# Conditioning slices of a two-layer hybrid backbone: where their bias is loaded and where the odd layer sums them

## The chip, the cores and the metric

The kernel runs on one core of a Trainium2 chip. The number is the device time of one execution in microseconds (us), and the time before is the median of three executions. A core has five engines with a queue of instructions each: TensorE (PE, with its weight loads PEld), VectorE (DVE), ScalarE (ACT), GpSimd (POOL) and SyncE (SP). An engine works through its queue in order. Transfers run on 16 DMA engines; in this kernel SP issues the large loads and POOL the small ones, those that spread a row over partitions, and the indirect ones.

## The reference, cut to what matters

```
for l in range(2):
    sh1, sc1, g1, sh2, sc2, g2 = split(silu(c) @ ada_w[l] + ada_b[l], 6)
    u = rmsnorm(x, norm1_g[l]) * (1 + sc1) + sh1
    y = even_mixer(u, u_ctx, ...) if l == 0 else odd_mixer(u, ...)
    x = x + g1 * (y @ w_out[l])
    x = x + g2 * hier_moe(rmsnorm(x, norm2_g[l]) * (1 + sc2) + sh2, ...)
```

512 tokens of width 1024, in fp32. The even mixer is neighbourhood attention beside a short gated convolution; the odd mixer is Hyena (two long convolutions, each with a gate) beside a Conformer convolution with a layer norm. The MoE picks one of four groups and two of its four experts. `ada_w[l]` is 1024 x 6144: the six conditioning slices of a layer cost 24 MB of weights for one vector c (the context's vector goes through layer 0 beside it), and of them the gate g1 and the three of the MoE are wanted only when the mixer's out-projection ends.

## The kernel before, in words

The program is written for a framework that orders each engine's instructions itself, by a timeline that it estimates, with the order of the program text as priority. So an instruction can move in its engine's queue when others around it do.

**Projections.** A weight chunk of 128 x 1024 is loaded (`raw`), split into a high part by a cast on ACT (`whi`, line 141) and the rest by a subtraction on DVE (`wlo`, line 142), and every product is three matmuls (`mm3`, lines 155 to 157). `proj_ch` makes 128 channels for all 512 tokens, 24 matmuls. The parts lie in a pool `wp` of four slots each.

**Conditioning.** The slices are made in pairs j = 0, 1, 2 of 2048 columns. `ada` does a pair with matmuls. `ada_sums` does it without PE: for each half h of the columns, eight loads of 512 KB are multiplied by a column of silu(c) and added up on DVE into `adaacc` (lines 245 and 247), and two matmuls with a column of ones per half then sum the partitions into a PSUM tile `ps` (line 253). After the second half `ada_done` adds the bias (line 266, tile `adar`), multiplies in a norm's gain (line 311), and stores four rows to DRAM (`adad`, line 271). For layer 0 pairs 1 and 2 go this way, between the attention's query projections; for layer 1 pairs 1 and 2, as a generator `fill` of 20 steps (ten a pair: two loads and their additions are a step, the products end a step, the last step is the bias and the store). In layer 1 the loads (`adaw`) take `whi` and `wlo` slots of `wp`.

**The bias tile.** After the last product the bias is loaded by POOL into a tile `adab` of tag `t2` (lines 256 to 258; 128 x 512, each of four rows spread over 32 partitions). Tag `t2` has four buffers, which the norm's `y` tiles and others use too.

**The odd layer's order.** `ORDER` (line 63) is a list of steps: `p`, `v`, `x` are Hyena projections with a short convolution, `c` a Conformer block (two projections, the gate `sg`, a shifted copy `wide` by 16 transfers at line 815, 31 matmuls at line 819), `A` and `B` long convolutions (transforms at lines 629 and 800), `L` the layer norm; `t` followed by a number takes that many steps of `fill`. In the list before, 18 of the 20 steps come ahead of `B0` and the last two after `B1`.

**What waits for the last pair.** `mid` (line 938) loads the stored rows again, spread over the partitions, by POOL (`bcast`, line 317): g1b and b2b for the residual, a2b and g2b from pair 2, and `ab` (line 973) for the router. `evac` (lines 1018 and 1019) adds g1 times the out-projection to the residual `xr`; line 997 scales it by a2b for the MoE (`hm`); `wa` (line 981) is the router's weight scaled by pair 2, which the logits (line 1037) need; line 1026 transposes `xr` for them.

Of the kernel before, what the change touches and what calls it, by code (L numbers as in the profile page):

```python
# [8 lines left out]
F32 = mybir.dt.float32  # L9
# [37 lines left out]
FW = [0.5, 0]  # L47
GD = 0
DE = [[], []]
BK = 0  # L50
PB = (4, 2, 2)
SX = 1
FB = 4
# [6 lines left out]
PM = 1  # L60
PU = [[], []]
FIRST = (640, 128)
ORDER = 'p1 t1 v1 t1 v0 t1 p0 t1 c0 t2 A0 v3 t1 v2 t1 p2 t1 c2 t2 p3 t1 c1 t2 A1 x0 t1 c3 t2 x1 t1 B0 x2 L0 x3 B1 t9'
TWO_PI = (6.28125, 0.0019350051879882812, float(2.0 * math.pi - 6.28125 - 0.0019350051879882812))
P_, Q_ = (0, 1, 2, 3), (4, 5, 6, 7)
NP1, NP2, NQ2, NQ3 = 8, 9, 10, 11
# [2 lines left out]
class Build:  # L69
# [83 lines left out]
    def mm3(self, ps, lh, ll, rh, rl, first, last):  # L153
        nc = self.nc
        nc.tensor.matmul(ps, lh, rh, start=first, stop=False)  # L155
        nc.tensor.matmul(ps, lh, rl, start=False, stop=False)  # L156
        nc.tensor.matmul(ps, ll, rh, start=False, stop=last)  # L157

    def proj_tok(self, uh, ul, W, t, ks=range(8), at=8, mid=None):

# [10 lines left out]
    def proj_ch(self, uh, ul, w, c0, lo_engine=None):  # L171

        v3 = lambda r: r.rearrange("p (k c) -> p k c", k=8)
        raw = self.raw_load(w[c0 // 128])
        wh, wl = self.split(v3(raw), lo_engine)
        ps = self.mmt()
        for k in range(8):
            self.mm3(ps, wh[:, k, :], wl[:, k, :], uh[k], ul[k], k == 0, k == 7)
        return ps

    def rstd(self, ss, n, eps, name):
# [25 lines left out]
    def ada(self, l, j):  # L207

        nc, A = self.nc, self.A
        b = A["ada_b"]  # L210
        ps = self.mmt()
        for k in range(8):
            if k == BK:
                bias = self.wk.tile([128, 512], F32, tag="t2", name="adab")
                nc.gpsimd.dma_start(bias, bass.AP(tensor=b.tensor, offset=b.offset + l * 6144 + j * 2048,
                                                  ap=[[512, 4], [0, 32], [1, 512]]))
            raws = []
            for h in range(2):
                raws.append(self.spare.pop(0) if self.spare else self.rawp.tile([128, 1024], F32, tag="raw", name="raw"))
                if self.spare:  # L220
                    self.spare.append(raws[-1])
                c0 = j * 2048 + h * 1024
                nc.sync.dma_start(raws[-1], A["ada_w"][l, k * 128:k * 128 + 128, c0:c0 + 1024])
            for g in range(4):
                nc.tensor.matmul(ps[32 * g:32 * g + 32, :], self.cT[:, k, :],
                                 raws[g // 2][:, (g % 2) * 512:(g % 2) * 512 + 512], start=(k == 0), stop=(k == 7))
            yield
        self.ada_done(l, j, ps, bias)

    def ada_sums(self, l, j):  # L230

        nc, A = self.nc, self.A
        b = A["ada_b"]
        for h in range(2):
            acc = self.ep2.tile([128, 1024], F32, tag="adaacc", name="adaacc", bufs=1)
            c0 = j * 2048 + h * 1024
            for k in range(8):
                if l and j:
                    raw = self.wp.tile([128, 1024], F32, tag=("whi", "wlo")[k % 2], name="adaw")
                else:  # L240
                    raw = self.spare.pop(0)
                    self.spare.append(raw)
                nc.sync.dma_start(raw, A["ada_w"][l, k * 128:k * 128 + 128, c0:c0 + 1024])
                if k == 0:
                    nc.vector.tensor_scalar(acc, raw, self.cT[:, k, 0:1], None, op0=ALU.mult)
                else:
                    nc.vector.scalar_tensor_tensor(acc, raw, self.cT[:, k, 0:1], acc, op0=ALU.mult, op1=ALU.add)
                if k % 2:
                    yield
            if not h:  # L250
                ps = self.mmt()
            for g in (2 * h, 2 * h + 1):
                nc.tensor.matmul(ps[32 * g:32 * g + 32, :], self.onec.to_broadcast([128, 32]), acc[:, (g % 2) * 512:(g % 2) * 512 + 512],
                                 start=True, stop=True)
            if not h:
                yield
        bias = self.wk.tile([128, 512], F32, tag="t2", name="adab")
        nc.gpsimd.dma_start(bias, bass.AP(tensor=b.tensor, offset=b.offset + l * 6144 + j * 2048,
                                          ap=[[512, 4], [0, 32], [1, 512]]))
        self.ada_done(l, j, ps, bias)  # L260
        yield

    def ada_done(self, l, j, ps, bias):
        nc, A = self.nc, self.A
        rows = self.ep2.tile([128, 512], F32, tag="adar", name="adar", bufs=1)
        nc.vector.tensor_tensor(rows, ps, bias, op=ALU.add)
        if j == 0:
            self.gain_rows(A["norm1_g"], l, 64, rows)
        elif j == 2:
            self.gain_rows(A["norm2_g"], l, 0, rows)  # L270
        nc.sync.dma_start(self.adad[l][j], rows[0:128:32, :])
        if j == 0:
            self.cols[l] = self.cp.tile([128, 16, 1], F32, name=f"adac{l}")
            nc.sync.dma_start(self.cols[l].rearrange("p a o -> p (a o)"),
                              self.adad[l][j].rearrange("a (q p) -> p (a q)", p=128))
# [549 lines left out]
    def odd(self, st):  # L825
# [82 lines left out]
        fill = self.ada1  # L908
        for w in ORDER.split():
            if w[0] == "t":  # L910
# [669 lines left out]
```

## Time and profile before

| | us |
|---|---|
| median of three executions (lowest, highest) | 1089.05 (1087.94, 1095.08) |
| the profiled execution's own time | 1094.75 |
| its span in the trace | 1092.9 |
| PE busy | 994.9 |
| DVE busy | 799.6 |
| ACT busy | 500.0 |
| POOL busy | 237.4 |

The span leaves 1.85 us of the profiled execution's time outside. Times in the trace count from the start of the span. The mean granted clock of TensorE is 0.947 of full speed: the clock falls to half in stretches, mostly behind a wait of PE. The odd layer runs up to about 840 us and the second MoE from there on.

### The profile page before, as it was taken

The page shows a single profiled execution, that of the slowest core. Times are in us where ns is not written, and L with a number is a line of the kernel's source. Part 1 is how long each engine was busy: PE and PEld are TensorE (multiplying, and loading weights), DVE is VectorE, ACT ScalarE, POOL GpSimd, SP SyncE. Part 2 cuts the span into 40 slices and gives each one's busy share as a digit, 9 for nine tenths or more (in the row PEclk, how much of TensorE's full clock was granted, in tenths as well). Part 3 has the DMA queues.
Part 4 walks back from the last instruction along what each step waited for, and adds up shares of the span by engine and source line. Part 5 has one row for each costly group of instructions (what it writes and reads, how often), then busy time and mean ns, then how long its engine had stood idle before and what let it go on. Part 6 is the DMA issues. An engine that isn't in the chain of part 4 may idle for free.

```text
span 1092.9 us, 14537 instructions
## 1 busy us (share of the span) xinstructions
PE 994.9 (91%) x5070; PEld 747.1 (68%) x5070; DVE 799.6 (73%) x1215; ACT 500.0 (46%) x786; POOL 237.4 (22%) x245
## 2 busy tenths in 40 slices
PE   6999999989995899999977999998998949999995
PEld 4787777667884677777755757566576837777663
DVE  3584588487368798898958787867755368988894
ACT  4342313477244576568624413212153137676562
POOL 2030313011343232353320000000011131333221
PEclk8999989989998899999988999998989779999998
DMA  9965783752624779999645755636227685799885
GB/s 350 345 215 161 245 277 116 267 182 95 214 93 175 260 244 340 309 313 299 195 148 195 256 153 175 201 79 211 77 100 241 241 289 194 242 293 323 306 256 139
DMA packets 77989, 240.78 MB, mean 220 GB/s; under 512 B 17987, under 2 KB 19806, under 8 KB 77912
## 3 DMA queue, kind: packets, MB, share of 16 engines
q1 hardware_dynamic: 62488, 209.83, 55.6%
q0 software_dynamic: 15424, 29.98, 11.1%
q8 instruction: 41, 0.67, 0.3%
q14 instruction: 36, 0.29, 0.1%
HBM read 227.40 MB, written 25.73 MB: 232 GB/s over the span
## 4 chain that ended last, share of the span: by engine, by line
PE 69%; DMA 11%; DVE 10%; issue 5%; ACT 2%; SPq 1%; POOL 1%; POOLq 0%; DVEq 0%; ACTq 0%
PE mm L155 15%; PE mm L156 15%; PE mm L157 14%; PE mm L1420 4%; PE mm L819 4%; DVE wlo L142 3%; DMA adab<-in_ada_b 2%; PE tr L1372 2%; DMA adaw<-in_ada_w 2%; PE mm L629 2%; PE mm L575 1%; DMA raw<-in_moe 1%; DMA xe<-hd,gi 1%; PE sc L545 1%; PE sc L629 1%
## 5 line engine op out<-in xcount | busy, mean ns | idle before, releaser
L141 ACT CAST whi<-raw 128x1024 fp32r<-128x1024 f32 x199 | 206.3, 1051 | 146.4 <-PE mm L156 46.0
L142 DVE TENSOR_TENSOR wlo<-raw,whi 128x1024 fp32r<-128x1024 f32 x199 | 242.4, 1229 | 35.0 <-ACT whi L141 34.3
L155 PE MATMUL mm<-whi,xt 128*128 128x512 f32 x208 | 85.7, 412 | 0.5 <-ACT xt L1375 0.5
L156 PE MATMUL mm<-wlo,xt 128*128 128x512 f32 x208 | 84.1, 404 | 1.8 <-DVE wlo L142 1.5
L157 PE MATMUL mm<-whi,xt 128*128 128x512 f32 x208 | 82.8, 398 | 0.0
L1361 POOL DMA_INDIRECT xe<-hd,gi x34 | 44.0, 1293 | 115.8 <-PE tr L1372 101.5
L156 PE MATMUL mm<-u,whi 128*128 128x512 f32 x160 | 64.1, 401 | 2.0 <-DVE u L349 2.0
L155 PE MATMUL mm<-u,whi 128*128 128x512 f32 x160 | 63.9, 408 | 1.1 <-ACT u L345 0.7
L157 PE MATMUL mm<-u,wlo 128*128 128x512 f32 x160 | 63.2, 397 | 0.0
L1372 PE MATMUL tr<-ident,xe 128*128 128x128 f32 x264 | 41.4, 283 | 18.1 <-DMA xe<-hd,gi 17.7
L155 PE MATMUL mm<-whi,at 128*128 128x512 f32 x132 | 54.5, 447 | 3.7 <-ACT at L1434 2.9
L1452 DVE SCALAR_TENSOR_TENSOR eo<-mm,sw,gb 128x512 f32<-128x512 f32 x66 | 47.6, 744 | 9.3 <-PE mm L157 8.9
L156 PE MATMUL mm<-wlo,at 128*128 128x512 f32 x132 | 53.1, 416 | 0.0
L1453 POOL DMA_INDIRECT out<-eo,gi x17 | 32.9, 1936 | 85.7 <-DVE eo L1452 46.6
L1372 PEld LDWEIGHTS tr<-ident,xe 128*128 128x128 f32 x264 | 33.3, 146 | 26.6 <-issue 19.9
L157 PE MATMUL mm<-whi,at 128*128 128x512 f32 x132 | 50.8, 407 | 0.0
L1378 DVE TENSOR_TENSOR xt<-tr,xt 128x512 fp32r<-128x512 f32 x66 | 37.5, 570 | 17.4 <-ACT xt L1375 14.0
L1375 ACT CAST xt<-tr 128x512 fp32r<-128x512 f32 x66 | 32.5, 496 | 37.4 <-PE tr L1372 37.0
L755 POOL MEMSET pad<- 128x1 f32 x12 | 1.2, 98 | 217.0 <-DVE x L762 138.6
L156 PEld LDWEIGHTS mm<-wlo,xt 128*128 128x128 f32 x208 | 39.6, 190 | 12.6 <-DVE wlo L142 4.5
L1453 POOL DMA_INDIRECT xd<-eo,gi x16 | 34.2, 2136 | 56.8 <-DVE eo L1452 36.3
L155 PEld LDWEIGHTS mm<-whi,xt 128*128 128x128 f32 x208 | 39.5, 190 | 9.3 <-ACT xt L1375 1.4
(411 smaller groups left out, 2444.6 us busy)
## 6 DMA issues: line engine op xcount, KB each, us to landing
raw<-in_moe SPq DMA_DIRECT2D x142, 512.0 KB
mr<-in_moe SPq DMA_DIRECT2D x48, 512.0 KB
bias<-in_ada_w SPq DMA_DIRECT2D x32, 512.0 KB
adaw<-in_ada_w SPq DMA_DIRECT2D x32, 512.0 KB
raw<-in_w_in_odd SPq DMA_DIRECT2D x20, 512.0 KB
raw<-in_ada_w SPq DMA_DIRECT2D x16, 512.0 KB
raw<-in_w_out SPq DMA_DIRECT2D x16, 512.0 KB
raw<-in_w_qkv SPq DMA_DIRECT2D x12, 512.0 KB
```

The lines of the kernel that those rows point to most:

```text
L141: nc.scalar.copy(hi, raw3)
L142: (lo_engine or nc.vector).tensor_tensor(lo, raw3, hi, op=ALU.subtract)
L155: nc.tensor.matmul(ps, lh, rh, start=first, stop=False)
L156: nc.tensor.matmul(ps, lh, rl, start=False, stop=False)
L157: nc.tensor.matmul(ps, ll, rh, start=False, stop=last)
L819: nc.tensor.matmul(out[32 * g:32 * g + 32, :], w[:, q, g, :], wide[:, g, q:q + 512], start=(q == 0), stop=(q == 7))
L1361: self.fetched = self.nc.gpsimd.indirect_dma_start(out=xe, out_offset=None, in_=self.hd[l][:, :], in_offset=bass.IndirectOffsetOnAxis(ap=g ...
L1372: nc.tensor.transpose(pt[:, k * 128:k * 128 + 128], xe[:, (4 * h + k) * 128:(4 * h + k) * 128 + 128], self.ident)
L1378: nc.vector.tensor_tensor(xt[:, 1, 4 * h:4 * h + n, :].rearrange("p a b -> p (a b)"), pt[:, 0:n * 128], hi, op=ALU.subtract)
L1420: nc.tensor.matmul(ps, xf[:, k, :], raw[:, k, :], start=False, stop=(k == 1))
L1452: nc.vector.scalar_tensor_tensor(o[:, sl], ps, wt, g2b[:, sl], op0=ALU.mult, op1=ALU.mult)
L1453: nc.gpsimd.indirect_dma_start(out=self.dst[l][:, :], out_offset=bass.IndirectOffsetOnAxis(ap=di, axis=0), in_=o, in_offset=None, bounds_c ...
```

## The change

Three edits. First, the bias of a pair is loaded straight into the tile in which the rows will stand (`adar`, one buffer), by a POOL transfer that is issued when the pair is begun, ahead of its sums; line 266 then adds `ps` in place. The tile `adab` goes. Second, `mm3` returns its last matmul, `proj_ch` keeps the latest, and for layer 1 the products of a half are ordered behind that matmul (`issue_after`). Third, `ORDER` takes one more step after `A0`, after `A1` and at `x1`, so that all 20 are taken ahead of `B0`, and the nine after `B1` go.

```diff
-BK = 0
-ORDER = 'p1 t1 v1 t1 v0 t1 p0 t1 c0 t2 A0 v3 t1 v2 t1 p2 t1 c2 t2 p3 t1 c1 t2 A1 x0 t1 c3 t2 x1 t1 B0 x2 L0 x3 B1 t9'
+ORDER = 'p1 t1 v1 t1 v0 t1 p0 t1 c0 t2 A0 t1 v3 t1 v2 t1 p2 t1 c2 t2 p3 t1 c1 t2 A1 t1 x0 t1 c3 t2 x1 t2 B0 x2 L0 x3 B1'
...
     def mm3(self, ps, lh, ll, rh, rl, first, last):
-        nc.tensor.matmul(ps, ll, rh, start=False, stop=last)
+        return nc.tensor.matmul(ps, ll, rh, start=False, stop=last)
...
     def proj_ch(self, uh, ul, w, c0, lo_engine=None):
-            self.mm3(ps, wh[:, k, :], wl[:, k, :], uh[k], ul[k], k == 0, k == 7)
+            self.last_mm = self.mm3(ps, wh[:, k, :], wl[:, k, :], uh[k], ul[k], k == 0, k == 7)
...
     def ada_sums(self, l, j):
-        b = A["ada_b"]
+        bias = self.ada_bias(l, j)
...
-            for g in (2 * h, 2 * h + 1):
-                nc.tensor.matmul(ps[32 * g:32 * g + 32, :], self.onec.to_broadcast([128, 32]), acc[:, (g % 2) * 512:(g % 2) * 512 + 512],
-                                 start=True, stop=True)
+            with self.tc.issue_after(self.last_mm.ins) if l else ExitStack():
+                for g in (2 * h, 2 * h + 1):
+                    nc.tensor.matmul(ps[32 * g:32 * g + 32, :], self.onec.to_broadcast([128, 32]), acc[:, (g % 2) * 512:(g % 2) * 512 + 512],
+                                     start=True, stop=True)
...
-        bias = self.wk.tile([128, 512], F32, tag="t2", name="adab")
-        nc.gpsimd.dma_start(bias, bass.AP(tensor=b.tensor, offset=b.offset + l * 6144 + j * 2048,
-                                          ap=[[512, 4], [0, 32], [1, 512]]))
...
+    def ada_bias(self, l, j):
+        b = self.A["ada_b"]
+        bias = self.ep2.tile([128, 512], F32, tag="adar", name="adar", bufs=1)
+        self.nc.gpsimd.dma_start(bias, bass.AP(tensor=b.tensor, offset=b.offset + l * 6144 + j * 2048,
+                                               ap=[[512, 4], [0, 32], [1, 512]]))
+        return bias
...
     def ada_done(self, l, j, ps, bias):
-        rows = self.ep2.tile([128, 512], F32, tag="adar", name="adar", bufs=1)
+        rows = bias
```

`ada`, for pair 0 of layer 1, gets its bias from `ada_bias` in the same way. Line numbers of the changed kernel are one lower up to `ada`, four lower at the products (249), and the bias load is its line 259; lines from 266 on are unchanged.

The even layer, POOL's queue between the query projections (`rh` belongs to the head norm, `vs` is a copy of the values, `gainr` is a norm's gain), before:

```order
L188 TENSOR_TENSOR rh<-rh,mhalf 128x8 x6
L455 DMA vs<-vt 64x1536
L456 DMA vs<-vt 64x1536
L188 TENSOR_TENSOR rh<-rh,mhalf 128x8 x3
L258 DMA adab<-in_ada_b 128x1x512 x2
L309 DMA gainr<-in_norm_g 64x1x512
L215 DMA adab<-in_ada_b 128x1x512
```

and of the changed kernel:

```order
L259 DMA adar<-in_ada_b 128x1x512
L187 TENSOR_TENSOR rh<-rh,mhalf 128x8 x6
L455 DMA vs<-vt 64x1536
L456 DMA vs<-vt 64x1536
L187 TENSOR_TENSOR rh<-rh,mhalf 128x8 x2
L259 DMA adar<-in_ada_b 128x1x512
L187 TENSOR_TENSOR rh<-rh,mhalf 128x8
```

The first bias load has gone from behind nine of the head norms' operations to a place ahead of all of them; the second now waits for the single `adar` buffer, with a head norm's operation behind it.

The odd layer, PE's queue at the last products of pair 2 (line 253; the transforms of `B0` at 800 and 629, the last Conformer block at 819, then `x1`'s projection), before:

```order
L157 MATMUL mm<-u_5416,wlo 128x512
L800 MATMUL sc<-Di,T 128x128 x16
L629 MATMUL sc<-ur,D 128x256 x4
L253 MATMUL mm<-adaacc,onec 32x512 x2
L629 MATMUL sc<-ur,D 128x256 x12
L819 MATMUL mm<-wide,raw 32x512
```

and of the changed kernel, where they are line 249, the same transforms and then the end of `x1`'s projection:

```order
L156 MATMUL mm<-u_5413,wlo 128x512
L800 MATMUL sc<-Di,T 128x128 x16
L629 MATMUL sc<-ur,D 128x256 x16
L819 MATMUL mm<-wide,raw 32x512
L154 MATMUL mm<-u_5411,whi 128x512
```

```order
L819 MATMUL mm<-wide,raw 32x512 x29
L154 MATMUL mm<-u_5413,whi 128x512
L155 MATMUL mm<-u_5414,whi 128x512
L156 MATMUL mm<-u_5413,wlo 128x512
L249 MATMUL mm<-adaacc,onec 32x512 x2
```

The products have left the run of transforms ahead of the Conformer block and stand behind the block's matmuls and the first 12 of `x1`'s 24.

The end of the odd layer, DVE's queue (`seq` and `yc` are the layer norm's, `z` and `yz` the last long convolution's, `mm<-mm,gb` is line 1018 on the first tile of the out-projection), before:

```order
L903 TENSOR_TENSOR yc_6841<-y,yc_6840 128x512 x4
L142 TENSOR_TENSOR wlo<-raw,whi 128x1024
L760 SCALAR_TENSOR_TENSOR sc<-pad,hsw,sc 128x512
L762 SCALAR_TENSOR_TENSOR x_6492<-pad,hsw,sc 128x128x4
L870 TENSOR_TENSOR z<-x_6492,zt 128x32x16
L874 TENSOR_TENSOR yz<-z,yz 128x512
L266 TENSOR_TENSOR adar<-mm,adab 128x512
L311 SCALAR_TENSOR_TENSOR adar<-adar,gainr 64x512
L1018 TENSOR_TENSOR mm<-mm,gb 128x512
```

and of the changed kernel:

```order
L903 TENSOR_TENSOR yc_6852<-y,yc_6851 128x512 x4
L141 TENSOR_TENSOR wlo<-raw,whi 128x1024
L760 SCALAR_TENSOR_TENSOR sc<-pad,hsw,sc 128x512
L762 SCALAR_TENSOR_TENSOR x_6500<-pad,hsw,sc 128x128x4
L870 TENSOR_TENSOR z<-x_6500,zt 128x32x16
L874 TENSOR_TENSOR yz<-z,yz 128x512
L141 TENSOR_TENSOR wlo<-raw,whi 128x1024
L1018 TENSOR_TENSOR mm<-mm,gb 128x512
L1019 TENSOR_TENSOR xr<-xr,mm 128x512
L981 TENSOR_TENSOR wa<-wr,ab 128x160
```

Lines 266 and 311 are gone from between the last long convolution and line 1018: in the changed kernel they stand 20 rows up, ahead of the layer norm. In their place is the first split (`wlo`) of the out-projection's second half, and `wa` follows the first `evac`, where before it came behind four splits and two scalings.

## Rows read from the trace of the kernel before

**Rows 1.** The page: busy time by engine; the chain that ended last.

```profile
PE 994.9 (91%) x5070; PEld 747.1 (68%) x5070; DVE 799.6 (73%) x1215; ACT 500.0 (46%) x786; POOL 237.4 (22%) x245
...
PE 69%; DMA 11%; DVE 10%; issue 5%; ACT 2%; SPq 1%; POOL 1%; POOLq 0%; DVEq 0%; ACTq 0%
```

**Rows 2.** Tile `adab`: what its users waited for, who waited (us, times).

```profile
  DMA adab<-in_ada_b: 14.0, 2
...
  PE mm L155: 3.1, 1
```

**Rows 3.** Windows: busy us of each engine (instructions), granted clock, DMA share, GB/s.

```profile
146.00:227.00 81.00, 81.00 (x459) 57.86 (x458) 60.36 (x79) 34.04 (x56) 15.43 (x30) 1.00 0.65 228
...
750.00:800.00 50.00, 45.75 (x231) 29.16 (x229) 36.91 (x43) 12.72 (x19) 0.25 (x4) 0.93 0.37 117
...
845.00:865.00 20.00, 17.93 (x75) 14.76 (x76) 8.81 (x14) 3.37 (x7) 2.99 (x2) 0.67 0.88 345
...
960.00:1020.00 60.00, 59.45 (x271) 44.83 (x270) 52.86 (x68) 41.95 (x63) 19.06 (x13) 1.00 0.97 300
```

**Rows 4.** The chain that ended last, four pieces: start us, us, what.

```profile
124.69 13.41 DMA adab<-in_ada_b
...
752.15 6.23 DMA adaw<-in_ada_w
...
817.47 12.44 DMA adab<-in_ada_b
...
833.78 7.47 DMA gb<-ada
```

**Rows 5.** Timeline of DVE: start, us, line, [idle before, releaser]; even layer, odd layer's end.

```profile
129.02 1.21 DVE L142 TENSOR_TENSOR wlo<-raw,whi 128x1024 fp32r<-128x1024 f32 x1
138.13 0.69 DVE L266 TENSOR_TENSOR adar<-mm,adab 128x512 f32<-128x512 f32 x1 [7.89 <-DMA adab<-in_ada_b]
...
829.93 0.69 DVE L266 TENSOR_TENSOR adar<-mm,adab 128x512 f32<-128x512 f32 x1 [6.10 <-DMA adab<-in_ada_b]
...
841.27 1.29 DVE L997 TENSOR_TENSOR hm<-xr,gb 128x512 f32<-128x512 f32 x2 [6.00 <-DMA gb<-ada]
```

**Rows 6.** Timeline of PE in the even layer, around the first bias.

```profile
135.24 0.39 PE L156 MATMUL mm<-ul,whi 128*128 128x512 f32 x1
135.47 0.39 PE L157 MATMUL mm<-ul,wlo 128*128 128x512 f32 x1
138.96 0.77 PE L155 MATMUL mm<-ul,whi 128*128 128x512 f32 x1 [3.11 <-DVE adar L266]
...
144.92 0.39 PE L157 MATMUL mm<-ul,wlo 128*128 128x512 f32 x1
```

**Rows 7.** Timeline of PE in the odd layer: transforms, and the sums' last products.

```profile
718.71 3.62 PE L629 MATMUL sc<-ur,D 128*128 128x256 f32 x16
...
759.81 1.92 PE L253 MATMUL mm<-adaacc,onec 128*32 128x512 f32 x4 [3.25 <-DVE adaacc L247]
761.66 7.54 PE L629 MATMUL sc<-ur,D 128*128 128x256 f32 x24
```

**Rows 8.** Timeline of SP: the last Conformer block's shifted copy.

```profile
752.75 11.22 SPq L815 DMA_DIRECT2D wide<-sg  x16
```

**Rows 9.** Timeline of PE across the end of the out-projection.

```profile
840.10 0.39 PE L157 MATMUL mm<-whi,yz 128*128 128x512 f32 x1
...
855.25 4.25 PE L1037 MATMUL sc<-wa,xT 128*128 128x20 f32 x32
859.33 0.77 PE L155 MATMUL mm<-whi,yc 128*128 128x512 f32 x1
...
868.76 0.47 PE L155 MATMUL mm<-whi,yc 128*128 128x512 f32 x1
...
875.63 0.47 PE L155 MATMUL mm<-whi,yc 128*128 128x512 f32 x1
```

**Rows 10.** Timeline of POOL at the end of the odd layer.

```profile
833.78 1.06 POOL L317 DMA_DIRECT2D gb<-ada  x2 [8.79 <-DVE mm L1018]
```

More of the change, by code (lines that the diff above doesn't have):

```diff
@@ L209, in ada @@
         nc, A = self.nc, self.A
-        b = A["ada_b"]
+        bias = self.ada_bias(l, j)
         ps = self.mmt()
         for k in range(8):
-            if k == BK:
-                bias = self.wk.tile([128, 512], F32, tag="t2", name="adab")
-                nc.gpsimd.dma_start(bias, bass.AP(tensor=b.tensor, offset=b.offset + l * 6144 + j * 2048,
-                                                  ap=[[512, 4], [0, 32], [1, 512]]))
             raws = []
@@ L232, in ada_sums @@
         nc, A = self.nc, self.A
-        b = A["ada_b"]
+        bias = self.ada_bias(l, j)
         for h in range(2):
@@ L251, in ada_sums @@
                 ps = self.mmt()
-            for g in (2 * h, 2 * h + 1):
-                nc.tensor.matmul(ps[32 * g:32 * g + 32, :], self.onec.to_broadcast([128, 32]), acc[:, (g % 2) * 512:(g % 2) * 512 + 512],
-                                 start=True, stop=True)
+            with self.tc.issue_after(self.last_mm.ins) if l else ExitStack():
+                for g in (2 * h, 2 * h + 1):
+                    nc.tensor.matmul(ps[32 * g:32 * g + 32, :], self.onec.to_broadcast([128, 32]), acc[:, (g % 2) * 512:(g % 2) * 512 + 512],
+                                     start=True, stop=True)
             if not h:
                 yield
-        bias = self.wk.tile([128, 512], F32, tag="t2", name="adab")
-        nc.gpsimd.dma_start(bias, bass.AP(tensor=b.tensor, offset=b.offset + l * 6144 + j * 2048,
-                                          ap=[[512, 4], [0, 32], [1, 512]]))
         self.ada_done(l, j, ps, bias)
         yield
+    def ada_bias(self, l, j):
[4 more added lines that the diff above has]
+        return bias
     def ada_done(self, l, j, ps, bias):
         nc, A = self.nc, self.A
-        rows = self.ep2.tile([128, 512], F32, tag="adar", name="adar", bufs=1)
+        rows = bias
         nc.vector.tensor_tensor(rows, ps, bias, op=ALU.add)
```

## The prediction

> **What bounds the kernel now.** I read the page first. TensorE is busy for 91% of the span and carries 69% of the chain that ended last; DMA has 11% of it, DVE 10% [rows 1]. So a microsecond is won only where PE stands still or runs at its lower clock, and an edit that frees DVE or a queue counts only if PE waits there. The view of the tile `adab` comes next: only two of the five bias additions waited for their load, 14.0 us of DVE together, and PE waited for one of them directly, 3.1 us [rows 2]. Then the windows show whether PE is short of work where a gain would have to survive: behind the even-layer place it runs without a gap, 81.00 busy of 81.00 us at granted clock 1.00; at 750 to 800 it is busy 45.75 of 50 at clock 0.93; at 845 to 865 it is granted 0.67 of full speed; in the second MoE it is full again, with the DMA engines at a share of 0.97 [rows 3]. The chain of waits names what came last at each place: the bias load twice (13.41 and 12.44 us), a conditioning load (6.23), and a reload of the stored rows (7.47) [rows 4]. These places are the three terms.
>
> **Even layer.** Removed: a bias load issued at 124.69 that lands 13.41 us later [rows 4]. DVE's last other work starts at 129.02, and the addition then holds DVE's queue for 7.89 us, to 138.13 [rows 5]. PE needs the PSUM tile that this addition frees: its last matmul starts at 135.47, it idles 3.11 us, and from 138.96 to 144.92 it runs 14 matmuls 0.43 us apart, where they were 0.23 apart before the wait (135.24 to 135.47) [rows 6]. These are its two clocks, 1.2 and 2.4 GHz; the wait came first, the low clock behind it. Price: 3.11 + 14 x (0.426 - 0.227) = 3.1 + 2.8 = 5.9 us. The new load stands ahead of the head norms on POOL, so it has more than the 13.41 us it took. Bounds: 2.5, if PE then meets another wait short of this one (the queue of DVE behind the addition holds two splits and two sums that PE and SP want too) and pays the clock once more; 6 if nothing replaces it. PE's gapless 81 us behind it [rows 3] say that what is won there stays, so I stay near the upper end: **5**.
>
> The Trainium skill, page "DMA: Bandwidth & Descriptors", section "Anatomy of one DMA — SWDGE (gpsimd) path", fits a GpSimd transfer at 2.0 us plus its bytes over 436 GB/s; for this tile of 256 KB that is an estimate of 2.6 us. By it the load would land before DVE is free at 130.2, and moving it would be worth nothing. The trace disagrees with 13.41 and 12.44 us; it decides here, and the sum goes by it.
>
> **Odd layer, sums.** Three moves: sums' steps go ahead (20 of 20 before `B0`), the products stand behind a projection, and the bias no longer comes late. Before, the last products wait 3.25 us for DVE's sums in the midst of the transforms of `B0`, then take 1.92 us for four matmuls and 7.54 for 24 transforms; the same transforms took 3.62 for 16 at full clock, 0.226 each [rows 7]. So the price is 3.25 + 24 x (0.314 - 0.226) = 2.1, + half of 1.92 = 1.0: 6.3 us. What is late next: the Conformer block behind the transforms, whose `wide` copy takes SP 11.22 us from 752.75 [rows 8] and so ends at 764.0, with 5.2 to spare before the transforms end at 769.2. Nearly all of the 6.3 can therefore come through, at most about a microsecond being taken by that copy. Against it: the last bias addition and gain (two DVE operations of 0.69, as in [rows 5]) now stand ahead of the layer norm's chain, where PE has less to do: 1.3. Sum 6.3 - 1.3 = **5**. Ends: 0, if the early sums' loads (6.23 us on the chain at 752.15 [rows 4]) only make DVE wait earlier, ahead of `B0`'s own work; 6.5 if the norm's chain has slack. The DVE additions and loads themselves are neither more nor fewer; moved ahead by one to three steps they lie beside PE's projections, in a stretch where DVE is busy 36.91 of 50 us and the DMA share is 0.37 [rows 3]. If that cover were gone each would cost its load on PE's path, 6.23.
>
> **End of the odd layer.** Before, the bias of pair 2 is issued at 817.47, since its `t2` buffer is only then free, and lands at 829.9 [rows 4]. DVE idles 6.10 us for it; behind it in the queue stand both `evac` lines, then the scaling `hm`, which waits another 6.00 us for a2b [rows 5]: a2b is a reload of the rows that this addition makes, held on POOL for 8.79 us [rows 10], 7.47 us on the way [rows 4]. The four splits of the out-projection's second half and `wa` stand behind that in the same queue, as told with the order of the change, and PE waits for them. What is that worth on PE? The first half's last matmul ends at 840.3. Then the first tile of the second half, three groups of transposes and 32 logits fill the time to 859.33: 19.0 us. A whole tile of the same work (24 matmuls, 4 transposes, 8 logits) takes 875.63 - 868.76 = 6.87 at full clock; the other 24 logits 24/32 x 4.25 = 3.2 [rows 9]; two groups of transposes some 1.0 by the difference of such tiles. So 11.1 of the 19.0 is work, 7.9 waiting and low clock. The tile after it took 868.76 - 859.33 = 9.43 against 6.87: 2.6 more at low clock. Together 10.5. In the changed order the first split and `wa` no longer have anything late ahead of them, and the remaining splits stand ahead of `hm`; a2b's reload may come when it will. What is late next: buffers for the splits, which PE's own first half frees, and the reload g1b for the first `evac`; the one is paced by PE, the other was there before 831. Bounds: 4, if the splits arrive only when the first half ends and PE still pays a wait and its clock; 13 if also the wait of `evac` for g1b shrinks and the routing behind comes earlier by it. I take **11**, nearest to the row.
>
> The store of pair 2 (SP) and the second bias load each pass other entries: on SP the store moves ahead of the last weight load and of the residual's, which costs these one issue that nobody waits for, and frees the MoE's loads that were queued behind it; the bias load now waits at the head of POOL's queue for the rows of pair 1 to be stored, with paddings of the short convolutions behind it. That row of POOL which waited 8.79 us with `ab` behind it [rows 10] is what such a wait looks like; here the paddings have slack as long as the store goes out when its rows are ready.
>
> The Trainium skill speaks against this move in the same section: a DMA's semaphore wait is paid on the issuing sequencer before dispatch, so an early issue is a wait for all that follows. The trace agrees (8.79 us on POOL); whether it costs PE here no row of before shows.
>
> **Sum.** 5 + 5 + 11 = 21 us. Against the profiled execution that is 1094.75 - 21 = 1073.8; its surplus over the median of the three (5.7 us) I take to be in both, so from 1089.05 the forecast is **1068**. The second MoE, limited by DMA at 0.97 [rows 3], could take back an earlier start, but its loads are bounded by buffers that the stages before it free, so they start earlier too.
>
> **Rivals.**
> 1. Only the end pays. The attention and the projections around both sums are re-ordered too, and what PE gains at the two places returns as other waits (a raw load, the `wide` copy): 11 us, 1078. For: the DMA engines are busy at the even place, and the scheduler moves more than the diff. Against: the gapless 81 us.
> 2. The end's wait is replaced. Splits wait for buffers, a2b lands beside the MoE's loads (share 0.88 [rows 3]) and the routing waits for `hm` instead: the end gives 4, the rest 6 of 10: 1079. For: 7.47 us for a reload of 1 MB shows those queues loaded.
> 3. Slower: DVE held in queue order by the early sums. Each addition of a conditioning load stands ahead of a long convolution's own DVE work; where the load is late by the 6.23 us of [rows 4], PE stops that long and pays 2.1 of low clock behind: 8.3 a time. At two such places the odd and even gains are gone and half of the end's; at four (each `A0`, `A1`, `B0` and the last Conformer block) it is 33 - 16 = 17 us slower, 1106. Against: DMA share 0.37 there.
> 4. The move does nothing: the second bias and the order move, yet the reload path (store, a2b) keeps PE waiting as before, and the even wait returns at the next PSUM tile: 1086.
>
> **How the numbers follow.** Forecast (gain 15 to 26) 0.60, rival 1 0.15, rival 2 0.13, rival 3 0.05, rival 4 0.07. About 1%, 10.9 us, is what a measurement of this kernel can tell from no change: below 1078.2 is faster. The forecast and half of rivals 1 and 2 lie below it: 0.60 + 0.14 = 0.74. Same: the other half, rival 4 and a part of rival 3's weaker form, 0.21. Slower: 0.05. Range: low from the upper ends, 6 + 6.5 + 13 = 25.5, with a microsecond for the scatter between executions: 1062; high takes in rivals 1 and 2 with 2 us more: 1081. Rivals 3 and 4 and the forecast's tail stay out, under 2 in 10. The forecast's own range is 1063 to 1074.
>
> **What the changed profile would show.** Even: no DVE wait for the bias, no PE gap near 136, no run of 0.43 us behind it. Odd: the products in `x1`'s projection without a wait, the 24 transforms near 5.4 us, the Conformer block from about 763. End: DVE's idle time before `evac` under 2 us or put down to g1b, `wa` ahead of the third split, tiles of the second half near 6.9 us each. Wrong would be: DVE waiting for `adaw` ahead of a long convolution, POOL waiting for the store with a short convolution behind it, or PE at half clock in the second half still; or the MoE's loads ending when they did before.

## The result, and the profile after

The changed kernel takes 1077.86 us (median of 13 runs) against 1089.23 of before in the same sessions: ratio 0.990, interval 0.9876 to 0.9923. That is 11 us where 21 were forecast: inside the stated range of 1062 to 1081, outside the forecast's own of 1063 to 1074, half of the sum. The profiled executions differ by 14.5 us (1094.75 and 1080.21); that of before stands 5.5 above its median, that of the change 2.4.

The page of the changed kernel, busy time and the chain's engines, answering to [rows 1]:

```profile
PE 985.7 (91%) x5070; PEld 740.1 (69%) x5070; DVE 802.1 (74%) x1215; ACT 500.2 (46%) x786; POOL 240.5 (22%) x245
...
PE 68%; DMA 15%; DVE 7%; issue 5%; ACT 2%; POOL 1%; SPq 1%; POOLq 0%; DVEq 0%; ACTq 0%
```

Tile `adar` of the changed kernel, which now takes the bias: what its users waited for, and the time from issue to landing of the two of its five loads for which the trace has a landing, answering to [rows 2]:

```profile
  DMA ada<-adar: 12.1, 2
...
DMA to landing us min/median/max: 5.6/8.5/11.5
```

No addition waits for a bias any more. Two loads wait on POOL for the store of the rows before (12.1 us together). Behind the longer of these waits, 7.5 us at 673, stand the paddings of a short convolution, which the prediction had named as a sign of being wrong; no engine waits for POOL there. The loads have not become quick, only early: the two took 5.6 and 11.5 us.

Windows of the changed kernel (columns as in [rows 3]; the first is moved by 6 us and the last by 10, to keep the same work in them):

```profile
140.00:221.00 81.00, 80.86 (x459) 57.66 (x457) 60.62 (x80) 34.07 (x56) 17.08 (x31) 1.00 0.68 240
750.00:800.00 50.00, 47.51 (x258) 31.35 (x257) 39.07 (x47) 14.54 (x22) 1.08 (x7) 1.00 0.34 98
845.00:865.00 20.00, 20.00 (x107) 16.90 (x106) 12.63 (x33) 4.97 (x10) 2.38 (x4) 1.00 0.69 208
950.00:1010.00 60.00, 59.94 (x276) 45.46 (x275) 53.67 (x69) 41.05 (x61) 19.19 (x13) 1.00 0.97 309
```

The middle two had clocks of 0.93 and 0.67 and gaps; both are at 1.00, and the second has no gap left. PE's timeline shows why in the odd layer (against [rows 7]: 7.54 us for 24 transforms, 3.25 of waiting) and at its end (three tiles of the out-projection's second half, 6.87 apart, against [rows 9]):

```profile
760.77 5.50 PE L629 MATMUL sc<-ur,D 128*128 128x256 f32 x24 [0.83 <-ACT b L632]
766.21 1.05 PE L819 MATMUL mm<-wide,raw 128*32 128x512 f32 x2
...
846.22 0.47 PE L154 MATMUL mm<-whi,yc 128*128 128x512 f32 x1
...
853.10 0.47 PE L154 MATMUL mm<-whi,yc 128*128 128x512 f32 x1
...
859.96 0.47 PE L154 MATMUL mm<-whi,yc 128*128 128x512 f32 x1
```

DVE of the changed kernel at the end of the odd layer, against [rows 5]: the first `evac` waits 1.02 us for PE, and `wa` starts 24.5 us earlier than before, in the change and before:

```profile
822.91 0.70 DVE L1018 TENSOR_TENSOR mm<-mm,gb 128x512 f32<-128x512 f32 x1 [1.02 <-PE mm L156]
823.64 0.69 DVE L1019 TENSOR_TENSOR xr<-xr,mm 128x512 f32<-128x512 f32 x1
824.91 0.33 DVE L981 TENSOR_TENSOR wa<-wr,ab 128x160 f32<-128x160 f32 x1 [0.59 <-DMA ab<-ada]
```

```profile
849.42 0.32 DVE L981 TENSOR_TENSOR wa<-wr,ab 128x160 f32<-128x160 f32 x1
```

So all three terms came. The larger part of what was lost again stands at a place of which the prediction has no term, the odd layer's first Conformer block. SP, PE and the chain of the changed kernel there:

```profile
616.97 0.33 SPq L131 DMA_DIRECT2D raw<-in_w_in_odd  x1
617.90 0.80 SPq L238 DMA_DIRECT2D adaw<-in_ada_w  x2
619.39 13.17 SPq L815 DMA_DIRECT2D wide<-sg  x16
```

```profile
632.18 1.03 PE L819 MATMUL mm<-wide,raw 128*32 128x512 f32 x1 [5.25 <-DMA wide<-sg]
...
687.34 1.02 PE L819 MATMUL mm<-wide,raw 128*32 128x512 f32 x2 [1.14 <-DMA wide<-sg]
```

```profile
618.32 8.65 DMA adaw<-in_ada_w
...
630.07 1.97 DMA wide<-sg
```

Two conditioning loads leave 1.5 us ahead of the shifted copy; the copy takes SP 13.17 us, and PE waits 5.25 us for it. SP and PE of the kernel before, where the copy took 10.49 us and PE waited 1.88:

```profile
621.93 10.49 SPq L815 DMA_DIRECT2D wide<-sg  x16
```

```profile
632.09 0.59 PE L819 MATMUL mm<-wide,raw 128*32 128x512 f32 x1 [1.88 <-DMA wide<-sg]
```

PE was 3.3 us ahead of before on entering the block and stands 3.5 behind when the second copy arrives. Of these 6.9 us (68.8 - 61.9 in the table below), 3.4 are the longer wait for the first copy and 1.1 a wait for the second, which before had none. Behind the longer wait the clock is low; the windows from there on, before and in the change:

```profile
632.00:690.00 58.00, 57.67 (x294) 39.75 (x294) 48.15 (x52) 15.64 (x22) 1.14 (x7) 1.00 0.57 175
```

```profile
632.00:690.00 58.00, 56.16 (x281) 38.26 (x282) 47.40 (x51) 16.61 (x23) 1.12 (x7) 0.96 0.53 156
```

A granted clock of 0.96 over 58 us is worth some 2.3 us, an estimate, so the three make up nearly all of the 6.9.

**Stages.** To compare runs I cut the trace at instructions that every kernel has. *Even*: start of the first attention scores. *Block 0*: from the first `ur` cast of `A0` (ACT) to the first matmul on the second copy. *Sums*: from the first matmul on the third copy to that on the fourth; the transforms of `B0` and before the change the sums' last products lie in it. *Norm*: from there to the layer norm's root (POOL). *End*: from the root to the second group of the router's counts (line 1240, tile `mm`). Each number is a difference of two start times in one profile, in us; the last column is the median and the interval of the ratio to before in the same sessions.

| kernel | even | block 0 | sums | norm | end | time, ratio |
|---|---|---|---|---|---|---|
| before | 188.8 | 61.9 | 46.5 | 37.0 | 79.8 | 1089.23 |
| the change | 182.7 | 68.8 | 40.3 | 36.6 | 67.2 | 1077.86, 0.988-0.992 |
| bias_only | 182.0 | 61.8 | 46.2 | 34.4 | 76.1 | 1087.05, 0.994-1.000 |
| order_only | 186.6 | 72.4 | 42.2 | 36.4 | 68.6 | 1081.09, 0.985-0.995 |
| bias_order | 182.7 | 68.3 | 40.6 | 54.1 | 67.2 | 1094.16, 1.0005-1.007 |
| no_a0 | 181.7 | 61.8 | 40.0 | 38.2 | 67.3 | 1068.86, 0.976-0.986 |
| no_a0_again | 183.2 | 61.8 | 40.0 | 36.5 | 67.3 | 1068.98, 0.979-0.986 |
| a0_only | 186.6 | 73.2 | 40.6 | 35.0 | 78.3 | 1093.62, 1.002-1.007 |
| a0_after_wide | 183.0 | 65.7 | 40.2 | 36.8 | 67.1 | 1077.98, 0.988-0.995 |
| a0_pool | 182.8 | 66.6 | 40.2 | 36.4 | 67.4 | 1074.69, 0.981-0.989 |
| no_a0_nohold | 183.1 | 61.8 | 39.8 | 51.1 | 68.5 | 1087.58, 0.997-1.001 |
| no_a0_latebias | 188.2 | 61.9 | 40.0 | 36.5 | 67.3 | 1072.94, 0.981-0.988 |
| bias_nogain | 182.7 | 61.8 | 48.2 | 35.4 | 67.2 | not compared |

### The profile page after: what moved, and what is told of

Its sections match the earlier page's. It is cut to its first block, busy times and chain, and to the rows that moved or that the text cites. A ratio compares the mean times of both kernels' runs of the same rounds, so it can differ in the third digit from the quotient of the medians.

```text
span 1078.4 us, 14533 instructions
## 1 busy us (share of the span) xinstructions
PE 985.7 (91%) x5070; PEld 740.1 (69%) x5070; DVE 802.1 (74%) x1215; ACT 500.2 (46%) x786; POOL 240.5 (22%) x245
## 4 chain that ended last, share of the span: by engine, by line
PE 68%; DMA 15%; DVE 7%; issue 5%; ACT 2%; POOL 1%; SPq 1%; POOLq 0%; DVEq 0%; ACTq 0%
PE mm L154 15%; PE mm L155 15%; PE mm L156 15%; DMA out<-eo,gi 9%; PE mm L819 4%; PE mm L1420 3%; PE tr L1372 2%; PE mm L629 2%; DVE wlo L141 2%; DMA xe<-hd,gi 1%; DMA xd<-eo,gi 1%; PE mm L575 1%; PE sc L545 1%; PE sc L629 1%; PE sc L800 1%
## 5 line engine op out<-in xcount | busy, mean ns | idle before, releaser
L154 PE MATMUL mm<-whi,xt 128*128 128x512 f32 x208 | 86.8, 417 | 0.5 <-ACT xt L1375 0.5
L156 PE MATMUL mm<-whi,xt 128*128 128x512 f32 x208 | 84.0, 404 | 0.0
L1361 POOL DMA_INDIRECT xe<-hd,gi x34 | 48.1, 1416 | 113.4 <-PE tr L1372 92.6
L155 PEld LDWEIGHTS mm<-wlo,xt 128*128 128x128 f32 x208 | 40.3, 194 | 13.0 <-DVE wlo L141 4.7
L154 PEld LDWEIGHTS mm<-whi,xt 128*128 128x128 f32 x208 | 40.2, 193 | 9.5 <-ACT xt L1375 1.4
L1453 POOL DMA_INDIRECT xd<-eo,gi x16 | 34.1, 2134 | 56.2 <-DVE eo L1452 36.4
```

The lines of the kernel that those rows point to most:

```text
L156: return nc.tensor.matmul(ps, ll, rh, start=False, stop=last)
L1361: self.fetched = self.nc.gpsimd.indirect_dma_start(out=xe, out_offset=None, in_=self.hd[l][:, :], in_offset=bass.IndirectOffsetOnAxis(ap=g ...
L1453: nc.gpsimd.indirect_dma_start(out=self.dst[l][:, :], out_offset=bass.IndirectOffsetOnAxis(ap=di, axis=0), in_=o, in_offset=None, bounds_c ...
```

## The experiments

**bias_only: the early load alone**, steps and products as before.

```diff
-ORDER = '... A0 t1 v3 ... A1 t1 x0 t1 c3 t2 x1 t2 B0 x2 L0 x3 B1'
+ORDER = '... A0 v3 ... A1 x0 t1 c3 t2 x1 t1 B0 x2 L0 x3 B1 t9'
-            with self.tc.issue_after(self.last_mm.ins) if l else ExitStack():
```

> The early bias load alone, with the steps and the products where they were before. Theory A (the three edits act at three places that add up, and the loss at the first Conformer block belongs to the step that was put behind A0): PE is 6 us ahead of before at 150 us, about 3 ahead at 600 and still about 3 ahead at 650, since the first shifted copy waits no longer than the 1.9 us of before; the last products still wait some 3 us for the sums and about 2 us of low clock follow; at the end of the odd layer 9 to 12 us are won: 1074 to 1079. Rival B (that loss comes with the earlier arrival at the block, whatever brings it): PE waits about 5 us for the first shifted copy here too, 3 us behind before at 650, 1080 to 1084. Rival C (the end's gain is the order's): the end gains under 3 us, 1083 to 1087.

The even layer gains all (182.0), block 0 is untouched (61.8), but the end gives 3.7 of 12.6. Theory A had 9 to 12 there and was wrong; rival C had under 3. DVE of this run shows what holds the end now:

```profile
825.48 0.68 DVE L310 SCALAR_TENSOR_TENSOR adar<-adar,gainr 64x512 f32<-64x512 f32 x1 [4.28 <-DMA gainr<-in_norm_g]
...
835.72 1.29 DVE L996 TENSOR_TENSOR hm<-xr,gb 128x512 f32<-128x512 f32 x2 [6.44 <-DMA gb<-ada]
...
843.59 1.40 DVE L980 TENSOR_TENSOR wa<-wr,ab 128x160 f32<-128x160 f32 x1
```

The norm's gain, like the bias of before, is loaded late into a `t2` tile. POOL of this run issues it behind the reload of g1b and b2b:

```profile
813.67 1.15 POOL L316 DMA_DIRECT2D gb<-ada  x2 [10.48 <-issue]
814.82 0.72 POOL L308 DMA_DIRECT2D gainr<-in_norm_g  x1
```

The gain has taken the bias's place, and the reload of a2b behind it costs DVE 6.44 us where it cost 6.00. Whether the buffer or the entry ahead of it on POOL makes it late, this run does not separate.

Another loss lies outside the stages of the table. From the second copy to the third this run takes 42.8 us, before 38.9. SP and PE of this run at the third copy, which before took SP 11.27 us with a wait of PE of 0.35:

```profile
706.78 15.15 SPq L814 DMA_DIRECT2D wide<-sg  x16
```

```profile
721.61 1.88 PE L818 MATMUL mm<-wide,raw 128*32 128x512 f32 x2 [4.28 <-DMA wide<-sg]
```

Two conditioning loads leave 1.0 us ahead of this copy, and SP stands 4.6 us for their landing. So a copy can be held in this way with the old list of steps too.

**order_only: the list of steps alone**, with the bias late, in a `t2` tile.

```diff
-ORDER = '... A0 v3 ... A1 x0 t1 c3 t2 x1 t1 B0 x2 L0 x3 B1 t9'
+ORDER = '... A0 t1 v3 ... A1 t1 x0 t1 c3 t2 x1 t2 B0 x2 L0 x3 B1'
```

> The new list of steps alone, with the bias loaded late into its own tile as before. Theory A: no gain at 150 us; PE waits about 5 us for the first shifted copy and stands 6 us behind before at 650; at the end most of the gain is there, since the last pair is begun and done before the layer norm and the late load is hidden: 10 to 12 us won there: 1080 to 1085. Rival C' (the end's gain needs the early load): the end gains under 4 us, 1088 to 1094.

As theory A had it, the end gives 11.2 us and the sums give 4.3 without hold and early load; block 0 loses 10.5. POOL of this run shows the late load issued at 755.52, ahead of the norm, whose tiles share `t2`; before, it was issued at 817.47 [rows 4].

```profile
755.52 0.67 POOL L258 DMA_DIRECT2D adab<-in_ada_b  x1 [0.37 <-issue]
756.89 0.67 POOL L309 DMA_DIRECT2D gainr<-in_norm_g  x1 [0.70 <-issue]
```

**bias_order: the change without the hold.**

```diff
-            with self.tc.issue_after(self.last_mm.ins) if l else ExitStack():
```

> The change without the hold: products are free to go where the scheduler puts them, which is the transforms of B0 again. Theory A: the same as the change up to 750 us (about 5 us of waiting at the first shifted copy); the last products cost at most 1 us of waiting, since their sums end a step earlier than before, so 0 to 3 us slower than the change: 1078 to 1081. Rival D (the hold makes the odd layer's gain): the wait for the sums and the low clock return, 5 to 6 us slower than the change: 1083 to 1085.

Neither theory held: the run is 16 us slower than the change, and not by the wait for the sums (sums 40.6) but in the norm stage, 54.1. It was run again without the step behind A0:

**no_a0_nohold.**

> The best list (no step behind A0) without the hold. The order of PE then has the last products between the transforms of B0, and two of their 16 rows behind the last Conformer block and x2's projection, as in the run without the hold before. Theory G (the hold pays because the products otherwise push two transforms of B0 out of their place; their own wait is nothing): PE idles 10 us or more for DVE in the middle of B0 near 795, and the time is 12 to 20 us above that of the list with the hold: 1081 to 1089. Rival D (that run's loss belonged to the step behind A0): within 4 us of the list with the hold, 1068 to 1073.

Theory G held: the norm stage takes 51.1 us, and the time is 1087.58. DVE and PE of this run:

```profile
756.94 1.22 DVE L781 TENSOR_TENSOR ed<-Af,T 128x1024 f32<-128x1024 f32 x1
775.25 1.23 DVE L141 TENSOR_TENSOR wlo<-raw,whi 128x1024 fp32r<-128x1024 f32 x1 [17.09 <-ACT whi L140]
```

```profile
797.70 2.69 PE L799 MATMUL sc<-Di,T 128*128 128x128 f32 x11 [13.61 <-DVE T L789]
```

In both orders without the hold, PE's queue has the products among the transforms of `B0`, and four of their 32 matmuls (two of the 16 rows in the order) stand behind the Conformer block and `x2`'s projection; DVE's queue has a split for that projection in the middle of `B0`'s additions. DVE stands 17.09 us for the split's cast, and PE later 13.61 us for `B0`. `order_only` has no hold either, but in its order all 32 stay in place, and its norm stage is 36.4. So the hold pays for the order that it leads to, in the company of the early load; why the scheduler displaces the four otherwise was not looked into.

**no_a0: the change without its step behind A0**, and the same timed again.

```diff
-... c0 t2 A0 t1 v3 ...
+... c0 t2 A0 v3 ...
```

> The change without the extra step behind A0; the other two still bring all 20 ahead of B0. Theory A: the two conditioning loads no longer stand ahead of the first shifted copy, PE waits for it under 2.5 us instead of 5.25, and 5 to 6 us of the loss at 632 us are back: 1071 to 1074. Rival B: the wait stays near 5 us and the time at 1077 to 1079. Rival E: the loads that move back collide with the next copy instead, and the time is the same though the first wait is gone.

> The list without the step behind A0 once more, timed in more rounds for a narrower interval: 1067 to 1073, ratio 0.978 to 0.986.

Theory A held: block 0 takes 61.8 us, and the time is 1068.9 us in both runs, 2 below the range that theory A gave. It is the best kernel of the study: 0.979 to 0.986 of before in the second timing, 9 us below the change. The step was not needed, since the list of the change holds 21 steps for 20. SP and PE of this run, where the changed kernel had 13.17 and 5.25:

```profile
617.89 10.37 SPq L815 DMA_DIRECT2D wide<-sg  x16
```

```profile
627.90 0.59 PE L819 MATMUL mm<-wide,raw 128*32 128x512 f32 x1 [1.74 <-DMA wide<-sg]
```

**a0_only: the step behind A0 in the kernel before**, one fewer at the list's end.

> The kernel before with the one step behind A0 added (and one fewer at the list's end); bias late, products free. Theory A (the step's two conditioning loads stand in SP's queue ahead of the first shifted copy): PE waits 3.5 to 5.5 us for that copy instead of 1.9 and stands 4 to 7 us behind before at 650 us. Since the sums end a step earlier, the 3.25 us wait of the last products may be gone, which gives some of it back; the end stays as before, with the bias 10 us or more after its issue: 1089 to 1096. Rival B (the loss needs the earlier arrival or one of the other edits): wait near 1.9 us, level with before at 650, 1083 to 1088.

Block 0 loses 11.3 us (PE waits 4.92 us for the copy) without any other edit; the sums give 5.9, since they end a step earlier. So rival B falls, and the sums' gain needs one step of the list, not the hold. Some 4 of the 11.3 have another cause. DVE and PE of this run in `A1`:

```profile
677.75 0.69 DVE L266 TENSOR_TENSOR adar<-mm,adab 128x512 f32<-128x512 f32 x1 [3.26 <-DMA adab<-in_ada_b]
```

```profile
688.08 3.52 PE L629 MATMUL sc<-ur,D 128*128 128x256 f32 x8 [3.84 <-DVE Af L635]
```

The step also brings the late bias of pair 1 ahead of the sums of `A1` in DVE's queue. `order_only` pays the same (4.09 us); `bias_order`, which differs from it in the early bias alone, does not, and its block 0 takes 68.3 us where that of `order_only` takes 72.4. So beside this step the early bias is worth some 4 us in the odd layer too.

**a0_after_wide: the step's two loads held behind the first copy.**

```diff
+                with self.tc.issue_after(self.wide_dma.ins) if (l, j, h) == (1, 1, 1) and k in (2, 3) else ExitStack():
+                    nc.sync.dma_start(raw, A["ada_w"][l, k * 128:k * 128 + 128, c0:c0 + 1024])
...
+                self.wide_dma = nc.sync.dma_start(wide[32 * i:32 * i + 32, g, a:b], sg[32 * g:32 * g + 32, a - at:b - at])
```

> The change with its step behind A0, but this step's two loads ordered behind the transfers of the first shifted copy. Theory A: the wait for that copy falls under 2.5 us and the time to that of the list without the step, 1068 to 1073. Rival F (it is not the two loads ahead of the copy but what the step does to the slots of the split weights, or its additions on DVE): the wait stays at 4 us or more, 1076 to 1080.

The wait for the first copy falls to 1.96 us, as theory A says, but the next copy now takes 12.90 us on SP and PE waits there:

```profile
629.14 0.59 PE L820 MATMUL mm<-wide,raw 128*32 128x512 f32 x1 [1.96 <-issue]
...
684.55 1.02 PE L820 MATMUL mm<-wide,raw 128*32 128x512 f32 x2 [3.75 <-DMA wide<-sg]
```

The time is that of the change, so the place was right and the remedy was not: what rival E expected of `no_a0`, a collision with the next copy, happens in this run.

**a0_pool: the step's two loads issued by POOL.**

```diff
+                q = nc.gpsimd if (l, j, h) == (1, 1, 1) and k in (2, 3) else nc.sync
+                q.dma_start(raw, A["ada_w"][l, k * 128:k * 128 + 128, c0:c0 + 1024])
```

> The change with its step behind A0, but this step's two loads issued by POOL, whose queue does little there, instead of SP. Theory J (SP's queue: a weight load waits 8.4 us at its head for a buffer, the conditioning loads behind it leave just ahead of the first shifted copy, and the copy's issue waits for them to land): SP's order ahead of the copy is that of before, so the wait for the copy is under 2.5 us, 1069 to 1074. Rival K (the DMA engines are short of time there, whoever issues): the copy is 3 us late as in the change, 1076 to 1080.

The result lies between the two theories: PE waits 3.47 us, block 0 takes 66.6, and the time is 1074.69. What SP waits for, in this run from 612 to 636 us (total, times, longest):

```profile
SPq L131 <- DVE wlo L141: 9.1, 1, 9.1
SPq L816 <- DMA adaw<-in_ada_w: 1.6, 1, 1.6
```

The extra loads are out of SP's queue, and still a weight load stands 9.1 us at its head until a split frees its buffer, and the next step's two conditioning loads leave behind it, just ahead of the copy. The change has the same (8.4 us); before, a weight load and two conditioning loads had gone 6 us ahead of the copy. What the extra step takes by the program, whoever issues its loads, is two slots of `whi` and `wlo`, and the cast of the next chunk, at 610.03 before, comes at 614.64 in the change, although PE is 3 us earlier. That the slots are what delays the cast is not shown: no run changed them alone. ACT of the kernel before, then ACT and DVE of the changed kernel:

```profile
610.03 1.06 ACT L141 CAST whi<-raw 128x1024 fp32r<-128x1024 f32 x1 [3.02 <-PE mm L156]
```

```profile
614.64 1.04 ACT L140 CAST whi<-raw 128x1024 fp32r<-128x1024 f32 x1
```

```profile
615.71 1.23 DVE L141 TENSOR_TENSOR wlo<-raw,whi 128x1024 fp32r<-128x1024 f32 x1 [2.90 <-ACT whi L140]
```

**no_a0_latebias: the best list and the hold, with the bias late.**

> The best list and the hold, with the bias loaded late into its own tile as before. Theory H (the early load is worth the even layer's wait and nothing at the end, where the order alone brings the last pair ahead of the norm): PE stops for the bias near 136 us as before, 2 to 6 us are lost there, the end is as with the early load: 1071 to 1076. Rival C (the end needs the early load too): DVE waits for the bias at the end, 1079 to 1085.

Theory H held: PE waits 3.80 us for the bias in the even layer, and the end keeps 67.3. The time is 4 us above the best by the medians, 2 to 4 by the ratios (0.9845 against 0.981 and 0.982), and the intervals overlap.

**bias_nogain: the early bias alone, without the gain of layer 1's last pair.**

> The early bias alone, with the norm's gain of layer 1's last pair left out (it is not loaded and not multiplied in). Theory L (with the early bias alone the end is still held by the gain's load, which waits for a t2 buffer as the bias did): the router's weight comes right behind the first evac and the end stage, from the layer norm's root to the router's counts, is 9 us or more shorter than in the run of the early bias alone, near 67 us as in the change. Rival M (the end needs the steps ahead of B0): the stage stays near 76 us. The routing sees other numbers, so only that stage is compared, not the whole time.

Theory L held: the end takes 67.2, that of the change, with the old list of steps. Without the gain the router sees other numbers, so the whole time, 1191.63 us, says nothing here; only this stage is read from it.

## Why the prediction was right, and why half of the sum is missing

The measured time is inside the range because the range had room for rivals 1 and 2; the forecast's own range, 1063 to 1074, misses it. At its own place each term came in about its size, but two of the three came by the list of steps, where I had counted on the early bias and the hold. By the stages of the two profiles 25.3 us were won (6.1, 6.2, 0.4 and 12.6), and 6.9 went back in block 0 and 2.8 between the even layer's place and the odd layer. This leaves 15.6, against the 14.5 by which the profiles differ. The sum had neither loss. So the range held in part by luck.

**Even layer, 5.** Measured 6.1 (188.8 to 182.7), by the early load alone; all kernels with it stand at 181.7 to 183.2, those without at 186.6 to 188.8, so 3.4 is as possible as 7.1. "What is won there stays" did not hold fully: from this point to the odd layer's first cast the four kernels with a late bias take 431.7 to 433.1 us, those with an early one 434.5 to 436.2. Some 3 us by the means go back in the attention and the first MoE; no single wait of that size was found. At that cast the kernels with an early bias stand at 617.0 to 619.4 us and those with a late one at 618.3 to 621.9, 1.9 apart in the mean. So the even layer's gain is worth 2 to 4 us net (4 by the medians 1072.94 and 1068.9, whose intervals overlap), not 5.

**Odd layer's sums, 5.** Measured 6.2 in their stage and 0.4 more in the norm's, where 1.3 had been taken off. The size was right, but of the three moves that I gave it to, one does it: a step of the list alone gives 5.9 (a0_only), and without the hold the stage is as short (40.6 in bias_order). The hold's part, some 13 to 18 us of a displaced `B0`, was in no row of before and in no sentence of the prediction.

**End, 11.** Measured 12.6. The cause was wrong in part: I gave it to the bias that no longer comes late, but the early load alone brings 3.7, since the gain's load is then as late as the bias was (67.2 without that gain); the list alone, which brings both loads ahead of the norm, gives 11.2.

**The step that failed** is the sentence that the additions and loads, moved ahead by one to three steps, "lie beside PE's projections, in a stretch where DVE is busy 36.91 of 50 us and the DMA share is 0.37". That stretch is 750 to 800 us; the step behind `A0` falls at 605 to 632, which it does not cover. There, by the trace, a split comes later, behind it a weight load, behind that two conditioning loads, and these hold the copy: 6.9 us. That the step as a whole is the cause is shown by `no_a0` and `a0_only`. Rival 1 had named the `wide` copy as a wait that could come, and its time (1078) is the one measured; but the end is not the only place that pays, and the loss is at neither of its two places. Rival 3 had early steps in the way of the odd layer on DVE; a wait of PE of that kind came only with a late bias, and for the bias (`a0_only`, `order_only`). Without the step behind `A0` the measured time is 1068.9, where the forecast was 1068; this is nearer than the terms were, since the even layer gives less than its 5 and the other two more than their 16 (6.6 and 12.6 in the change).

The Trainium skill, "DMA: Bandwidth & Descriptors", section "Anatomy of one DMA — SWDGE (gpsimd) path", puts a DMA's wait for a semaphore on the issuing sequencer, before dispatch. The trace agrees, on SP rather than on POOL where I had looked for it: 8.4 us at the queue's head, with two loads behind. The estimate of 2.6 us for the bias by its fit is reached in no run: the loads with a recorded landing took 5.1 to 16.6 us, and in the change, issued early and with nobody waiting, 5.6 and 11.5.

One more reading bears on the copy. The thirteen profiles hold 52 shifted copies. Where a conditioning load had been issued under 2 us ahead of the first transfer, 14 times, SP stood for such loads to land in 12, for 0.6 to 4.6 us. Where none had been issued in the 5.5 us ahead, 38 times, it never did, and the copy took 10.0 to 11.1 us but for one of 13.6.

Left open: why the copy's issue waits for conditioning loads to land at all (2.4 us in the change), although it touches neither their tiles nor their source; and how much each of slots and queue takes of the 6.9, since both remedies that were tried left more than half of it.

## What to carry to other kernels

Cost a step that is moved where it lands, queue by queue and slot by slot: the loads of one step too many, in buffers that a projection's weights share, cost more than the even layer's whole edit was worth. When a late load is found at the head of a wait, list what else is loaded as late for the same addition; here the gain took the bias's place. And time each edit alone: the largest gain belonged to another edit than the one that seemed to make it, and one edit with no term of its own in the sum was keeping off a loss of 13 to 18 us.

## What the runs showed of the hardware that was not expected

A load of 256 KB by POOL took 5.6 and 11.5 us in the change (two of five have a recorded landing), with nobody waiting for it, and 13.41 and 12.44 us before. Issued early it still takes several times the 1.2 us that its size would take at 223 GB/s, the mean rate on the page of the profile.

The first gather of the second MoE keeps PE idle for either 5.3 to 6.5 us (seven of the profiles) or 9.4 to 10.0 (six, those of before and of the change among them). It is some 4 us between profiles that no edit here explains. Both profiles of the one list that was profiled twice have the short wait; which of the two a kernel gets, and whether one kernel gets both, was not settled.
